# Reading the streamed operand of the weight products from two places in turn, in a two-layer decoder trunk

## The chip, the core and the metric

The kernel runs on one core of a Trainium2 chip. The metric is device time in microseconds (us) of one execution. The engines meant below are PE (TensorE, matrix products), DVE (VectorE), ACT (ScalarE), POOL (GpSimd) and SP, which issues the loads.

## What is computed

Two layers over 272 tokens (16 learned meta tokens ahead of 256 real ones) of width 2048, float32 throughout. Each layer adds a mixer and then a SwiGLU to the residual, each between two RMS norms; the meta tokens are dropped at the end.

```python
for l in range(DEPTH):                       # 2 layers
    hn = rms_norm(h, ln_mix_pre[l])
    mix = mixer_ab(hn, ...) if l % 2 == 0 else mixer_cd(hn, ...)
    h = h + rms_norm(mix, ln_mix_post[l])
    hn = rms_norm(h, ln_ffn_pre[l])
    h = h + rms_norm(swiglu(hn, ffn_w1[l], ffn_w3[l], ffn_w2[l]), ln_ffn_post[l])
return h[:, N_META:]
# swiglu: (silu(h @ w1) * (h @ w3)) @ w2, hidden width 5632
# mixer_ab: h @ w_in (7168 columns) -> gated linear recurrence | short convolution -> @ w_out
# mixer_cd: h @ w_in (4432 columns) -> gated recurrence | sparse attention -> @ w_out
```

## The kernel before

Features lie on the 128 partitions and tokens along the row. The residual is 16 tiles of 128 features by 272 tokens. A product with a weight matrix keeps a 128x128 block of the weight still in the array (the stationary operand) and streams the activations past it: one column of the array's input for each token, 272 of them, or 256 where the meta tokens aren't needed any more. The result goes to a PSUM bank in the order of the tokens.

Each float32 operand x is split into hi, its rounded form in the type fp32r that the array takes in one pass, and lo = x - hi. A product is then three: hi*hi, hi*lo and lo*hi, added up in PSUM. `group` issues them (L189 to L191) for the two 128-feature outputs of a 256-column piece of weight, over all 16 blocks of input features (or fewer for the second SwiGLU matrix). Weights are loaded by SP in pieces of 128x1024 and split by ACT (`whi`, L117) and DVE (`wlo`, L118).

The streamed activations are made in two places. `pre` makes `xh` (ACT) and `xl` (DVE) of the residual, block by block, at the start of each of the four stages (mixer, SwiGLU, mixer, SwiGLU), just ahead of the products that read them; `ahead` and `split_ahead` do the same for eight blocks whose products are issued before the norm is known. `split` makes the two parts of every other operand: gated outputs `og`, convolution outputs `yb`, attention `att`, recurrence `hc` and the SwiGLU's hidden blocks `hid`.

In layer 1 the second SwiGLU matrix is multiplied the other way round (`by_tokens`): the hidden block is the stationary operand, 128 tokens at a time, and the weights are streamed, 512 columns a product (256 for the last two pieces), so that tokens come out on the partitions. `output_part` adds the three partial sums, and `finish` normalizes each block of 128 tokens, adds the residual and stores it.

The order of PE's instructions is the order of the code; a scheduler orders the other engines.

Of the kernel before, what the change touches and what calls it, by code (L numbers as in the profile page):

```python
# [8 lines left out]
F32 = mybir.dt.float32  # L9
# [6 lines left out]
P = 128  # L16
NM = 16
# [24 lines left out]


class Trunk:


# [116 lines left out]
    def group(self, parts, xs, n, pump=0, hooks=None, before=None, between=None, begun=None):  # L163
# [7 lines left out]
        for ci, (k0, kc) in enumerate(self.chunks(parts, nk)):  # L171
# [3 lines left out]
            def products(i, kk):  # L175
# [92 lines left out]
    def spread(self, r, n):  # L268
# [5 lines left out]
        return ps  # L274

    def pre(self, k, lo_t, layer, which, update, xs):

# [57 lines left out]
    def start_stage(self, m, parts1, parts2, lo_t, layer, which, n, factors, update=None, between=None):  # L335
# [8 lines left out]
        def before(k):  # L344
            self.pre(k, lo_t, layer, which, update, xs)
            xg.append(tuple(x[:, nn - n :] for x in xs[k]))

# [24 lines left out]
    def split_ahead(self, m, layer, which, lo_t):  # L372

        nc = self.nc
        for k in range(4):
            g = self.gain(which, layer, k)
            for j, src in (2, self.h[k][:, lo_t:T]), (3, m["m"][k][:, : T - lo_t]):
                xh, xl = self.xhi[j][:, k, lo_t:T], self.xlo[j][:, k, lo_t:T]
                nc.scalar.activation(xh, src, AF.Copy, scale=g)
                nc.vector.scalar_tensor_tensor(xl, src, g, xh.bitcast(F32), op0=ALU.mult, op1=ALU.subtract)  # L380

    def ahead(self, m, parts, n, nn):
# [7 lines left out]
        def products():  # L390
            for accs, j in (near, 2), (far, 3):
                for k in range(kc):
                    xh, xl = self.xhi[j][:, k, T - n : T], self.xlo[j][:, k, T - n : T]
                    for (c, _), a in zip(outs, accs):
                        for i, (w, x) in enumerate(((hi, xh), (hi, xl), (lo, xh))):
                            nc.tensor.matmul(a[:, :n], lhsT=w[:, k, c : c + P], rhs=x, start=k + i == 0,  # L396
                                             stop=accs is far and k == kc - 1 and i == 2)
                            yield
# [359 lines left out]
    def mixer_ab(self, a, fetch, turn, update):  # L758
# [53 lines left out]
        for cp in range(4):  # L812
# [18 lines left out]
            for j in range(2):  # L831
                yb = ys[j]
                V.tensor_tensor(yb, accs[j][:, :T], yb, op=ALU.mult)
                ins[8 + 2 * cp + j] = self.split(yb, T, "yb")
        for hp in range(4):
# [10 lines left out]
            for j in range(2):  # L846
                o = normed[2 * hp + j]
                V.tensor_tensor(o, o, zs[j], op=ALU.mult)
                ins[2 * hp + j] = self.split(o, T, "og")
        order = list(range(8, 16)) + list(range(8))  # L850
        return self.project(a["ab_w_out"][0], [ins[i] for i in order], order, T, 0)

    def project(self, w, ins, order, n, layer):

        xs = [(h[:, :n], l[:, :n]) for h, l in ins]

# [13 lines left out]
    def swiglu(self, a, layer, lo_t, m, out=None):  # L870
# [17 lines left out]
        def hidden(zs, accs, hid):  # L888
# [5 lines left out]
            for y, z in zip(ys, zs):  # L894
                V.tensor_tensor(z, z, y, op=ALU.mult)
                h, l = self.split(z, n, "hid")
                hid.append((h[:, :n], l[:, :n]))

# [121 lines left out]
    def attend(self, h, q, k, vs, bias, out):  # L1020
# [37 lines left out]
        nc.tensor.matmul(last, lhsT=vC[:48, hc], rhs=few[:48].rearrange("p (b c) -> p b c", b=2), start=False, stop=True)  # L1058
        out[h] = self.split(po[:, :NL], NL, "att")
        yield  # L1060

    def mixer_cd(self, a, m):
# [27 lines left out]
        Rr = R[:, NM:T]  # L1090
        xr = [(h[:, NM:T], l[:, NM:T]) for h, l in xs]
        index_queries(accs1 + accs2)
# [79 lines left out]
        for g in range(2):  # L1172
            raw = self.fetch([(0, 0, wuv[:, 512 * g : 512 * (g + 1)].rearrange("(k p) c -> p k c", p=P))], 2, 512)
            hi, lo = self.whole(raw, 2, 512)
            for i, (t0, n) in enumerate(TOK[T]):
                ps = self.pp.tile([P, 512], F32, tag="ps", name="vacc")
                for kk in range(2):
                    ch, cl = cx[kk]
                    nc.tensor.matmul(ps[:n, :], lhsT=ch[:, t0 : t0 + n], rhs=hi[:, kk, :], start=kk == 0, stop=False)
                    nc.tensor.matmul(ps[:n, :], lhsT=ch[:, t0 : t0 + n], rhs=lo[:, kk, :], start=False, stop=False)  # L1180
                    nc.tensor.matmul(ps[:n, :], lhsT=cl[:, t0 : t0 + n], rhs=hi[:, kk, :], start=False, stop=kk == 1)
                c = slice(512 * g, 512 * (g + 1))
                S.copy(vs[i][32:48, c] if i == 2 else vs[i][:, c], ps[:n, :])
                if i == 1:
                    S.copy(vs[2][:NM, c], ps[:NM, :])
                self.pump(1)
# [8 lines left out]
        for g in range(4):  # L1195
# [11 lines left out]
            for c, y, t in both:  # L1207
# [3 lines left out]
                V.scalar_tensor_tensor(y, hs[c][:, NM:T], 0.5, y, op0=ALU.mult, op1=ALU.mult)  # L1211
                ins[c] = self.split(y, NL, "hc")
        self.flush()
# [5 lines left out]

    def by_tokens(self, w, row0, hid, c0, width, rounds, pump=0):  # L1220

        nk, step = len(hid), CH // width
        parts = {}
        for blocks in rounds:
            accs = [self.pp.tile([P, 512], F32, tag="ps", name="acc") for _ in blocks]
            for ci, k0 in enumerate(range(0, nk, step)):
                kc = min(step, nk - k0)
                if ci not in parts:
                    raw = self.fetch(self.cols(w, c0, width, row0)(k0, kc), kc, width)
                    parts[ci] = self.whole(raw, kc, width)  # L1230
                hi, lo = parts[ci]
                for kk in range(kc):
                    k = k0 + kk
                    for b, a in zip(blocks, accs):
                        xh, xl = (x[:, b * P : (b + 1) * P] for x in hid[k])
                        o = a[:, :width]
                        self.nc.tensor.matmul(o, lhsT=xh, rhs=hi[:, kk, :], start=k == 0, stop=False)  # L1237
                        self.nc.tensor.matmul(o, lhsT=xl, rhs=hi[:, kk, :], start=False, stop=False)  # L1238
                        self.nc.tensor.matmul(o, lhsT=xh, rhs=lo[:, kk, :], start=False, stop=k == nk - 1)  # L1239
                self.pump(pump)  # L1240
            yield from zip(blocks, accs)

    def turn(self, tiles, dst):
# [9 lines left out]
        yield  # L1253

    def output_part(self, a, layer, row0, hid, part, pi, out):

# [32 lines left out]
        def take(b, c, src):  # L1289
            t = part[2 * c + b][:, :half]  # L1290
            V.tensor_tensor(t, src, t, op=ALU.add)
            sq = self.slot("sq")
# [20 lines left out]
        for g in range(3):  # L1313
            for b, acc in self.by_tokens(w, row0, hid, 512 * g, 512, ((0, 1),), 1):
                if g + b == 0:
                    load_gain()
                for c in (2 * g, 2 * g + 1):
                    take(b, c, acc[:, half * (c % 2) : half * (c % 2 + 1)])
        self.flush()
# [42 lines left out]
```

## Time and profile before

| | |
|---|---|
| median of 3 runs | 2424.19 us (2424.02 to 2425.62) |
| the profiled execution's own time | 2426.06 us |
| its span, first to last instruction | 2424.3 us |
| PE busy | 2404.4 us (99%), 18563 matmuls |
| DVE, ACT, POOL busy | 61%, 45%, 4% of the span |
[...]

The profiled execution lies 1.87 us above the median; 1.76 us of its time lie outside its span. A matmul's busy time in the profile overlaps with its neighbours' (a 272-column one is shown as 0.29 us long while the next begins 0.125 us later), so the pace of PE is read from the starts of successive matmuls.

### The profile page before, as it was taken

What the parts mean: (1) busy time and instruction counts of PE and PEld (TensorE: products, weight loads), DVE (VectorE), ACT (ScalarE), POOL (GpSimd) and SP (SyncE); (2) the same over time, 40 slices, a digit from 0 to 9 for tenths busy, and PEclk for the clock granted to TensorE, in tenths of its full rate; (3) what the DMA queues carried; (4) which work ended last, traced back from release to release, by engine and by line L of the source; (5) the groups of instructions that cost most, each with busy time, mean ns of one, the idle gap of its engine ahead of it and who ended that gap; (6) DMA issues with size and microseconds to landing.
All of it is one profiled execution on the core that took longest, in us unless ns stands there. A gap on an engine that the chain in (4) does not pass through costs nothing.

```text
span 2424.3 us, 44974 instructions
## 1 busy us (share of the span) xinstructions
PE 2404.4 (99%) x18563; PEld 2331.7 (96%) x18563; DVE 1489.0 (61%) x2441; ACT 1096.4 (45%) x1628; POOL 107.3 (4%) x142
## 2 busy tenths in 40 slices
PE   9999999999999999999999999999999999999998
PEld 8999999999999999999999998999999899989997
DVE  7767566576554455455557788657755455555655
ACT  5333334454443334344355557555444444434443
POOL 1322100000000000000000000100000000000000
PEclk9999999999999999999999999999999999999999
DMA  8444455646555555565554744454666666666663
GB/s 256 144 143 131 146 159 174 183 124 199 174 177 177 177 175 166 174 187 178 166 170 145 210 123 142 146 183 148 210 190 186 190 190 186 189 191 187 187 196 100
DMA packets 402855, 416.97 MB, mean 172 GB/s; under 512 B 15551, under 2 KB 379562, under 8 KB 402650
## 3 DMA queue, kind: packets, MB, share of 16 engines
q1 hardware_dynamic: 402506, 413.95, 56.0%
q8 instruction: 145, 2.38, 0.4%
q14 instruction: 60, 0.49, 0.1%
q10 hardware_dynamic: 144, 0.15, 0.0%
HBM read 411.95 MB, written 2.10 MB: 171 GB/s over the span
## 4 chain that ended last, share of the span: by engine, by line
PE 65%; issue 30%; DVE 3%; DMA 1%; POOL 1%; ACT 1%; SPq 0%; ACTq 0%; DVEq 0%; POOLq 0%
PE acc L189 21%; PE acc L190 20%; PE acc L191 20%; PE lev L682 1%; POOL rms L263 0%; DVE xl L286 0%; DMA raw<-in_ab_w_in_dram 0%; DVE upd L419 0%; DVE wlo L118 0%; DVE h L420 0%; PE idx L992 0%; DVE preacc L314 0%; PE acc L396 0%; DVE wide L1310 0%; PE qk L1028 0%
## 5 line engine op out<-in xcount | busy, mean ns | idle before, releaser
L118 DVE TENSOR_TENSOR wlo<-raw,whi 128x1024 fp32r<-128x1024 f32 (+2 forms) x791 | 953.8, 1208 | 763.6 <-ACT whi L117 759.4
L117 ACT CAST whi<-raw 128x1024 fp32r<-128x1024 f32 (+2 forms) x791 | 817.1, 1035 | 1176.9 <-PE acc L190 862.1
L189 PE MATMUL acc<-xh,whi 128*128 128x272 f32 (+1 forms) x4248 | 1214.8, 286 | 0.5 <-DVE pt L536 0.3
L190 PE MATMUL acc<-xl,whi 128*128 128x272 f32 (+1 forms) x4248 | 1210.3, 285 | 0.6 <-DVE xl L286 0.2
L191 PE MATMUL acc<-xh,wlo 128*128 128x272 f32 (+1 forms) x4248 | 1206.7, 284 | 0.0
L189 PEld LDWEIGHTS acc<-xh,whi 128*128 128x128 f32 x4248 | 799.3, 188 | 5.0 <-ACT xh L285 0.8
L190 PEld LDWEIGHTS acc<-xl,whi 128*128 128x128 f32 x4248 | 797.5, 188 | 2.6 <-DVE xl L286 1.8
L191 PEld LDWEIGHTS acc<-xh,wlo 128*128 128x128 f32 x4248 | 797.6, 188 | 0.0
L189 PE MATMUL acc<-hidh,whi 128*128 128x272 f32 x704 | 202.9, 288 | 0.0
L190 PE MATMUL acc<-hidl,whi 128*128 128x272 f32 x704 | 202.6, 288 | 0.0
L191 PE MATMUL acc<-hidh,wlo 128*128 128x272 f32 x704 | 202.3, 287 | 0.0
L1237 PE MATMUL acc<-whi,hidh 128*128 128x512 f32 (+1 forms) x380 | 144.0, 379 | 0.0
L1239 PE MATMUL acc<-wlo,hidh 128*128 128x512 f32 (+1 forms) x380 | 143.3, 377 | 0.0
L1238 PE MATMUL acc<-whi,hidl 128*128 128x512 f32 (+1 forms) x380 | 143.2, 377 | 0.0
L190 PEld LDWEIGHTS acc<-hidl,whi 128*128 128x128 f32 x704 | 132.6, 188 | 0.0
L191 PEld LDWEIGHTS acc<-hidh,wlo 128*128 128x128 f32 x704 | 132.6, 188 | 0.0
L189 PEld LDWEIGHTS acc<-hidh,whi 128*128 128x128 f32 x704 | 132.5, 188 | 0.0
L1239 PEld LDWEIGHTS acc<-wlo,hidh 128*128 128x128 f32 x380 | 71.5, 188 | 14.3
L1238 PEld LDWEIGHTS acc<-whi,hidl 128*128 128x128 f32 x380 | 71.4, 188 | 13.7
L1237 PEld LDWEIGHTS acc<-whi,hidh 128*128 128x128 f32 x380 | 71.4, 188 | 13.7
L263 POOL TENSOR_TENSOR rms<-ms,minus_half 128x3 f32<-128x3 f32 (+1 forms) x8 | 16.1, 2014 | 1139.6 <-DVE ms L261 999.6
L892 DVE TENSOR_TENSOR y<-acc,scale 128x272 f32<-128x272 f32 (+1 forms) x88 | 35.1, 433 | 12.0 <-PE acc L191 12.0
(363 smaller groups left out, 2105.6 us busy)
## 6 DMA issues: line engine op xcount, KB each, us to landing
raw<-in_ffn_w_dram SPq DMA_DIRECT2D x518, 512.0 KB, 3.6
raw<-in_ab_w_in_dram SPq DMA_DIRECT2D x110, 512.0 KB, 3.6
raw<-in_cd_w_in_dram SPq DMA_DIRECT2D x68, 512.0 KB, 4.1
raw<-in_ab_w_out_dram SPq DMA_DIRECT2D x28, 512.0 KB, 3.6
raw<-in_cd_w_out_dram SPq DMA_DIRECT2D x28, 512.0 KB, 3.4
raw<-in_ffn_w_dram SPq DMA_DIRECT2D x17, 256.0 KB
raw<-in_ab_w_out_dram SPq DMA_DIRECT2D x8, 256.0 KB, 3.0
raw<-in_cd_w_out_dram SPq DMA_DIRECT2D x8, 256.0 KB, 2.8
```

What stands on the lines that cost most here:

```text
L117: nc.scalar.copy(hi[at], raw[at])
L118: nc.vector.tensor_tensor(lo[at], raw[at], hi[at].bitcast(F32), op=ALU.subtract)
L189: nc.tensor.matmul(o, lhsT=hi[:, kk, c : c + m], rhs=xh, start=k == 0, stop=False)
L190: nc.tensor.matmul(o, lhsT=hi[:, kk, c : c + m], rhs=xl, start=False, stop=False)
L191: nc.tensor.matmul(o, lhsT=lo[:, kk, c : c + m], rhs=xh, start=False, stop=k == nk - 1)
L263: i = self.nc.gpsimd.tensor_tensor(r[:, :w], self.ms[:, :w], self.minus_half[:, :w], op=ALU.pow)
L682: nc.tensor.matmul(ps[:M, j * half : (j + 1) * half], lhsT=k[:, j * P : j * P + M], rhs=upper(qh[:, j * P : (j + 1) * P]), start=True, sto ...
L892: V.tensor_tensor(y, accs[j][:, :n], R[:, :n], op=ALU.mult)
L1237: self.nc.tensor.matmul(o, lhsT=xh, rhs=hi[:, kk, :], start=k == 0, stop=False)
L1238: self.nc.tensor.matmul(o, lhsT=xl, rhs=hi[:, kk, :], start=False, stop=False)
L1239: self.nc.tensor.matmul(o, lhsT=xh, rhs=lo[:, kk, :], start=False, stop=k == nk - 1)
```

## The change

Two views are added. `pairs` is a row in its order, seen as pairs of neighbours; `woven` is a row that is seen as two halves, one element from each in turn.

Every streamed activation is now stored woven: tokens 0, 2, 4, ... in the first half of the row, 1, 3, 5, ... in the second. A product reads it through `woven`, so that tokens pass the array in their old order and PSUM is written as before; but each read is 136 elements of 4 bytes away from the one before (128 where the row has 256 tokens). ACT and DVE, which make `xh`, `xl` and the parts of `split`, now read 4-byte elements in order and write them to the two halves in turn; DVE also reads the hi part back from the two halves. Layer 1's hidden blocks, which are stationary there, stay in order; there the streamed weights are read in turn from the two halves of a 512-column piece (256 elements apart), so that the columns come out in another order, which the readers of PSUM undo with a step of two.

At the end of the program, after the last product of the second block of tokens, `forms` adds 50 products whose result nobody reads: five each of ten orders of reading 272, 256 or 512 columns of a weight piece.

```diff
+def pairs(t):
+    return t.rearrange("p (j a) -> p j a", a=2)
+def woven(t):
+    return t.rearrange("p (a j) -> p j a", a=2)
...
-                    o = a[:m, :n]
+                    o = a[:m, :n] if len(xh.shape) == 2 else pairs(a[:m, :n])
                     nc.tensor.matmul(o, lhsT=hi[:, kk, c : c + m], rhs=xh, start=k == 0, stop=False)
...
-    def split(self, src, n, name):
+    def split(self, src, n, name, weave=False):
...
-        self.nc.scalar.copy(hi[:, :n], src)
-        self.nc.vector.tensor_tensor(lo[:, :n], src, hi[:, :n].bitcast(F32), op=ALU.subtract)
+        if weave:
+            hi, lo, src = woven(hi[:, :n]), woven(lo[:, :n]), pairs(src)
+            at = slice(None)
+        else:
+            at = (slice(None), slice(0, n))
+        self.nc.scalar.copy(hi[at], src)
+        self.nc.vector.tensor_tensor(lo[at], src, hi[at].bitcast(F32), op=ALU.subtract)
...
+    def streamed(self, j, k, lo_t):
+        return (woven(x[j][:, k, :])[:, lo_t // 2 :, :] for x in (self.xhi, self.xlo))
...
-        xh, xl = self.xhi[k // 4][:, k % 4, lo_t:T], self.xlo[k // 4][:, k % 4, lo_t:T]
-        a = nc.scalar.activation(xh, h, AF.Copy, scale=g)
-        v = nc.vector.scalar_tensor_tensor(xl, h, g, xh.bitcast(F32), op0=ALU.mult, op1=ALU.subtract)
+        xh, xl = self.streamed(k // 4, k % 4, lo_t)
+        a = nc.scalar.activation(xh, pairs(h), AF.Copy, scale=g)
+        v = nc.vector.scalar_tensor_tensor(xl, pairs(h), g, xh.bitcast(F32), op0=ALU.mult, op1=ALU.subtract)
...
-                        o = a[:, :width]
-                        self.nc.tensor.matmul(o, lhsT=xh, rhs=hi[:, kk, :], start=k == 0, stop=False)
+                        o, wh, wl = pairs(a[:, :width]), woven(hi[:, kk, :]), woven(lo[:, kk, :])
+                        self.nc.tensor.matmul(o, lhsT=xh, rhs=wh, start=k == 0, stop=False)
...
+    def forms(self, hid):
...
+        far = lambda d, n: f[:, : 2 * d].rearrange("p (a j) -> p j a", a=2)[:, : n // 2, :]
+        for rhs, n in (
+            (f[:, 0:272], 272),
+            (far(128, 256), 256),
+            (far(136, 272), 272),
+            (far(256, 512), 512),
+            (far(240, 272), 272),
+            (far(160, 256), 256),
+            (far(130, 256), 256),
+            (f[:, 0:256].rearrange("p (a j) -> p j a", a=4), 256),
+            (f[:, 0:256].rearrange("p (a j c) -> p j a c", a=2, c=2), 256),
+            (f[:, 0:256].rearrange("p (a j c) -> p j a c", a=2, c=8), 256),
+        ):
...
+            for _ in range(5):
+                self.nc.tensor.matmul(o, lhsT=x, rhs=rhs, start=True, stop=True)
...
-                        src = acc[:, half * (c % 2) : half * (c % 2 + 1)]
+                        src = acc[:, c % 2 : 512 : 2]
...
         for b, acc in self.by_tokens(w, row0, hid, 7 * half, half, ((0,), (1,))):
             take(b, 7, acc[:, :half])
+            if b:
+                self.forms(hid)
             finish(b)
```

No instruction changes its place on any engine, apart from the 50 that are added. On DVE, at the start of layer 0's SwiGLU stage, the program before reads as follows; `upd` and `h` are the update of a residual block, `xl` its lo part.

```order
L419 TENSOR_TENSOR upd<-m,spread 128x272
L420 TENSOR_TENSOR h_121<-h_121,upd 128x272
L419 TENSOR_TENSOR upd<-m,bc 128x272 x2
L286 SCALAR_TENSOR_TENSOR xl<-h_121,pt_107,xh 128x272
L420 TENSOR_TENSOR h_122<-h_122,upd 128x272
```

The same place after the change:

```order
L439 TENSOR_TENSOR upd<-m,spread 128x272
L440 TENSOR_TENSOR h_121<-h_121,upd 128x272
L439 TENSOR_TENSOR upd<-m,bc 128x272 x2
L306 SCALAR_TENSOR_TENSOR xl<-h_121,pt_107,xh 128x136x2
L440 TENSOR_TENSOR h_122<-h_122,upd 128x272
```

Only the shape of `xl` differs: 136 pairs, one element of each in either half. On PE, the end of the program before is this (`acc` is the sum of the last 128x256 piece of the output):

```order
L1238 MATMUL acc<-whi,hidl 128x256
L1239 MATMUL acc<-wlo,hidh 128x256
L1237 MATMUL acc<-whi,hidh 128x256
L1238 MATMUL acc<-whi,hidl 128x256
L1239 MATMUL acc<-wlo,hidh 128x256
L1358 UNCONDITIONAL_BRANCH
```

After the change the same products are followed by the added ones:

```order
L1260 MATMUL acc<-whi,hidl 128x256
L1261 MATMUL acc<-wlo,hidh 128x256
L1301 MATMUL forms<-whi,hidh 128x272 x5
L1301 MATMUL forms<-whi,hidh 128x256 x5
L1301 MATMUL forms<-whi,hidh 128x272 x5
L1301 MATMUL forms<-whi,hidh 128x512 x5
L1301 MATMUL forms<-whi,hidh 128x272 x5
L1301 MATMUL forms<-whi,hidh 128x256 x25
L1411 UNCONDITIONAL_BRANCH
```

Nothing is queued behind them on PE.

## Rows read from the trace of the kernel before

**Rows 1.** The page: span and busy engines (us, share, instructions).
```profile
span 2424.3 us, 44974 instructions
PE 2404.4 (99%) x18563; PEld 2331.7 (96%) x18563; DVE 1489.0 (61%) x2441; ACT 1096.4 (45%) x1628; POOL 107.3 (4%) x142
```

**Rows 2.** Waits of PE: line, whom for, us in total, times, longest.
```profile
PE rgr L952 <- issue: 4.9, 1, 4.9
PE spread L272 <- POOL rms L263: 3.0, 3, 1.9
```

**Rows 3.** Timeline, 272-column products: start us, us, instruction.
```profile
999.72 0.29 PE L191 MATMUL acc<-hidh,wlo 128*128 128x272 f32 x1
...
1003.98 0.29 PE L189 MATMUL acc<-hidh,whi 128*128 128x272 f32 x1
```

**Rows 4.** Timeline, 512-column products followed by 256-column ones.
```profile
2384.79 0.39 PE L1237 MATMUL acc<-whi,hidh 128*128 128x512 f32 x1
...
2395.23 0.28 PE L1237 MATMUL acc<-whi,hidh 128*128 128x256 f32 x1
...
2400.03 0.28 PE L1239 MATMUL acc<-wlo,hidh 128*128 128x256 f32 x1
```

**Rows 5.** Timeline, a plain float32 product of 272 columns, in two passes.
```profile
156.94 0.62 PE L721 MATMUL o<-A,vt 128*128 128x272 f32 x2
157.40 0.41 PE L722 MATMUL o<-A,vt 128*128 128x144 f32 x2
```

**Rows 6.** Stretches of 100 us: engines' busy us (instructions), PE clock, DMA share, GB/s.
```profile
600.00:700.00 100.00, 100.00 (x802) 100.00 (x802) 55.20 (x74) 40.56 (x50) 0.00 (x0) 1.00 0.58 175
700.00:800.00 100.00, 100.00 (x802) 100.00 (x802) 43.38 (x40) 39.49 (x50) 0.00 (x0) 1.00 0.59 178
```

**Rows 7.** Groups of PE's matmuls by shape: count | busy us, mean ns.
```profile
L190 PE MATMUL acc<-xl,whi 128*128 128x272 f32 x2456 | 710.2, 289 | 0.2
...
L190 PE MATMUL acc<-xl,whi 128*128 128x256 f32 x1776 | 495.7, 279 | 0.3 <-DVE xl L286 0.2
...
L189 PE MATMUL acc<-hidh,whi 128*128 128x272 f32 x704 | 202.9, 288 | 0.0
...
L1237 PE MATMUL acc<-whi,hidh 128*128 128x512 f32 x324 | 128.3, 396 | 0.0
...
L189 PE MATMUL acc<-ogh,whi 128*128 128x272 f32 x128 | 37.1, 290 | 0.0
...
L1237 PE MATMUL acc<-whi,hidh 128*128 128x256 f32 x56 | 15.7, 281 | 0.0
```

**Rows 8.** Groups of DVE's instructions by shape, some with stepped operands.
```profile
L705 DVE TENSOR_TENSOR qh<-qh,F 128x136 f32<-128x136 f32 x24 | 9.5, 396 | 0.0
...
L687 DVE COPY_PREDICATED A<-lev,lev 126x128 f32<-126x128 uint8 x8 | 3.6, 452 | 6.6 <-PE lev L685 6.4
L671 DVE COPY_PREDICATED A<-lev,diag 128x128 f32<-128x128 uint8 x8 | 3.6, 446 | 0.0
...
L705 DVE TENSOR_TENSOR qh<-qh,f 128x136 f32<-128x136 f32 x8 | 2.6, 322 | 1.1 <-POOL A L646 1.1
...
L687 DVE COPY_PREDICATED A<-lev,lev 124x128 f32<-124x128 uint8 x8 | 2.4, 297 | 7.1 <-PE lev L685 6.9
```

**Rows 9.** One of six stretches of 25 us, and the sum over all six.
```profile
1675.00:1700.00 25.00, 24.86 (x209) 24.40 (x208) 25.00 (x60) 18.19 (x38) 0.00 (x0) 1.00 0.34 106
sum 150.00, PE 144.08 PEld 139.69 DVE 144.71 ACT 93.21 POOL 25.60; mean PE 24.01 PEld 23.28 DVE 24.12 ACT 15.53 POOL 4.27
```

**Rows 10.** Timeline: the last `xl` of a stage, and the products that first read it.
```profile
531.85 0.51 DVE L286 SCALAR_TENSOR_TENSOR xl<-h,pt,xh 128x272 fp32r<-128x272 f32 x1
...
536.74 0.29 PE L190 MATMUL acc<-xl,whi 128*128 128x272 f32 x1
```

**Rows 11.** Timeline: PE's last matmul, and the last instruction on DVE.
```profile
2414.96 0.28 PE L1239 MATMUL acc<-wlo,hidh 128*128 128x256 f32 x1
...
2419.70 0.74 DVE L1310 SCALAR_TENSOR_TENSOR wide<-m,rms,wide 128x512 f32<-128x512 f32 x1
```

More of the change, by code (lines that the diff above doesn't have):

```diff
@@ L345, in before @@
             self.pre(k, lo_t, layer, which, update, xs)
-            xg.append(tuple(x[:, nn - n :] for x in xs[k]))
+            xg.append(tuple(x[:, (nn - n) // 2 :, :] for x in xs[k]))
         accs1 = self.group(parts1, xg, n, before=before, between=between, begun=begun)
@@ L392, in products @@
                 for k in range(kc):
-                    xh, xl = self.xhi[j][:, k, T - n : T], self.xlo[j][:, k, T - n : T]
+                    xh, xl = self.streamed(j, k, T - n)
                     for (c, _), a in zip(outs, accs):
                         for i, (w, x) in enumerate(((hi, xh), (hi, xl), (lo, xh))):
-                            nc.tensor.matmul(a[:, :n], lhsT=w[:, k, c : c + P], rhs=x, start=k + i == 0,
+                            nc.tensor.matmul(pairs(a[:, :n]), lhsT=w[:, k, c : c + P], rhs=x, start=k + i == 0,
                                              stop=accs is far and k == kc - 1 and i == 2)
@@ L853, in project @@
     def project(self, w, ins, order, n, layer):
-        xs = [(h[:, :n], l[:, :n]) for h, l in ins]
+        xs = ins
         def cols(c0, width):
@@ L895, in hidden @@
                 V.tensor_tensor(z, z, y, op=ALU.mult)
-                h, l = self.split(z, n, "hid")
-                hid.append((h[:, :n], l[:, :n]))
+                hid.append(tuple(x[:, :n] for x in self.split(z, n, "hid")) if out is not None else self.split(z, n, "hid", True))
         for pi, (f0, f1) in enumerate(FPARTS):
@@ L1058, in attend @@
         nc.tensor.matmul(last, lhsT=vC[:48, hc], rhs=few[:48].rearrange("p (b c) -> p b c", b=2), start=False, stop=True)
-        out[h] = self.split(po[:, :NL], NL, "att")
+        out[h] = self.split(po[:, :NL], NL, "att", True)
         yield
@@ L1090, in mixer_cd @@
         Rr = R[:, NM:T]
-        xr = [(h[:, NM:T], l[:, NM:T]) for h, l in xs]
+        xr = [tuple(x[:, NM // 2 :, :] for x in both) for both in xs]
         index_queries(accs1 + accs2)
@@ L1178, in mixer_cd @@
                     ch, cl = cx[kk]
-                    nc.tensor.matmul(ps[:n, :], lhsT=ch[:, t0 : t0 + n], rhs=hi[:, kk, :], start=kk == 0, stop=False)
-                    nc.tensor.matmul(ps[:n, :], lhsT=ch[:, t0 : t0 + n], rhs=lo[:, kk, :], start=False, stop=False)
-                    nc.tensor.matmul(ps[:n, :], lhsT=cl[:, t0 : t0 + n], rhs=hi[:, kk, :], start=False, stop=kk == 1)
+                    o, wh, wl = pairs(ps[:n, :]), woven(hi[:, kk, :]), woven(lo[:, kk, :])
+                    nc.tensor.matmul(o, lhsT=ch[:, t0 : t0 + n], rhs=wh, start=kk == 0, stop=False)
+                    nc.tensor.matmul(o, lhsT=ch[:, t0 : t0 + n], rhs=wl, start=False, stop=False)
+                    nc.tensor.matmul(o, lhsT=cl[:, t0 : t0 + n], rhs=wh, start=False, stop=kk == 1)
                 c = slice(512 * g, 512 * (g + 1))
-                S.copy(vs[i][32:48, c] if i == 2 else vs[i][:, c], ps[:n, :])
+                S.copy(woven(vs[i][32:48, c] if i == 2 else vs[i][:, c]), pairs(ps[:n, :]))
                 if i == 1:
-                    S.copy(vs[2][:NM, c], ps[:NM, :])
+                    S.copy(woven(vs[2][:NM, c]), pairs(ps[:NM, :]))
                 self.pump(1)
@@ L1231, in by_tokens @@
                 hi, lo = parts[ci]
+                self.flat = hi.rearrange("p k c -> p (k c)")
                 for kk in range(kc):
@@ L1253, in turn @@
         yield
+    def forms(self, hid):
+        f = self.flat
+        x = hid[0][0][:, :P]
+        ps = self.misc("forms")
+        far = lambda d, n: f[:, : 2 * d].rearrange("p (a j) -> p j a", a=2)[:, : n // 2, :]
[11 more added lines that the diff above has]
+        ):
+            o = ps[:, :n]
+            if len(rhs.shape) == 3:
+                o = o.rearrange("p (j a) -> p j a", a=rhs.shape[2])
+            elif len(rhs.shape) == 4:
+                o = o.rearrange("p (j a c) -> p j a c", a=2, c=rhs.shape[3])
+            for _ in range(5):
+                self.nc.tensor.matmul(o, lhsT=x, rhs=rhs, start=True, stop=True)
     def output_part(self, a, layer, row0, hid, part, pi, out):
@@ L1290, in take @@
             t = part[2 * c + b][:, :half]
-            V.tensor_tensor(t, src, t, op=ALU.add)
+            if c < 6:
+                V.tensor_tensor(t, src, t, op=ALU.add)
+            else:
+                V.tensor_tensor(woven(t), pairs(src), woven(t), op=ALU.add)
             sq = self.slot("sq")
@@ L1317, in output_part @@
                 for c in (2 * g, 2 * g + 1):
-                    take(b, c, acc[:, half * (c % 2) : half * (c % 2 + 1)])
+                    take(b, c, acc[:, c % 2 : 512 : 2])
         self.flush()
```

16 lines of the change are left out of this document (8 added, 8 removed).

## The prediction, as it was put on record

> **What bounds the kernel.** I read the page first: PE is busy for 2404.4 of 2424.3 us [rows 1]. Then its waits: the longest is 4.9 us and the next sums to 3.0 [rows 2]. So the time is the number of matmuls times the pace at which PE starts them, and only that pace can move it by much. A matmul's shown duration overlaps with the next one, so the pace is read from starts. For 272 columns, 34 intervals lie between 999.72 and 1003.98: 125.3 ns each [rows 3]. For 512 columns there are 45 intervals from 2384.79 to 2395.23, 232.0 ns each, and for 256 columns 41 from there to 2400.03, 117.1 ns each [rows 4]. From 256 to 512 a column costs (232.0 - 117.1) / 256 = 0.449 ns, and 117.1 - 256 x 0.449 = 2.2 ns are fixed. [...]
>
> Is that another engine in the way? In the stretch 600 to 700 DVE is busy for 55.2 us and in 700 to 800 for 43.4, and both show the same 802 matmuls [rows 6]. So it isn't DVE; the two stretches move data alike, 175 and 178 GB/s. [...]
>
> **The change, part by part.**
>
> *The order of reading.* This is the term that decides. Counts: at 272 columns three groups of 2456 with `xh` and `xl`, three of 704 with `hid`, six of 128 (`og`, `yb`), together 10248; at 256 columns three of 1776, six of 128 (`att`, `hc`), three of 56, together 6264; at 512 columns three of 324, 972 [rows 7]. A rest of some 280 products is left out. At today's pace they take 10248 x 125.3 + 6264 x 117.1 + 972 x 232.0 ns = 1284.1 + 733.5 + 225.5 = 2243 us. No row shows PE reading single elements from two places in turn, so the price is bounded from both sides.
>
> [...] If the two are fetched independently, a column costs 0.417 ns and the fixed 2.2 stay: 115.5, 108.9 and 215.5 ns. The saving is 10248 x 9.8 + 6264 x 8.2 + 972 x 16.5 ns = 100.4 + 51.4 + 16.0 = 168 us.
>
> Upper end: if what is fetched for one place is lost at the switch to the other, each column pays for a fetch. The nearest rows with broken runs are DVE's: a predicated copy of 128 elements takes 297 ns with runs of four, but 452 with runs of two and 446 with single ones (L687, L671), 1.2 ns more an element [rows 8]. On PE that would be 0.449 + 1.2 = 1.65 ns a column, or 1.2 x (10248 x 272 + 6264 x 256 + 972 x 512) ns = 5870 us more.
>
> [...]
>
> I take the lower end. [...] But I hold this with little more than even odds.
>
> *Where DVE can't follow.* In six stretches of 25 us DVE is busy for 144.71 of 150 us [rows 9]: there it paces the kernel, or nearly, and a faster PE would wait. PE's 144 us in them don't shrink by 168 / 2243 = 7.5%: 10.8 us of the saving are not had.
>
> *Making the woven operands.* Some 160 instructions on DVE and as many on ACT now write in turn to two places. A DVE row with every second element in and out takes 322 ns for 136 elements, less than the 396 of the same line's forms with longer runs (L705), so the cost may be nothing; by the predicated copies it is 1.2 x 272 = 0.33 us an instruction at most [rows 8]. Where DVE is 61% busy or less this is hidden behind PE's products. In the four passes of `pre` it isn't wholly: 16 `xl` each, one for each block of features. The last `xl` of such a pass ends at 532.36 and is first read at 536.74, 4.4 us later [rows 10]. A faster PE eats 16 blocks x 12 products x 9.8 ns = 1.9 us of it, and 16 x 0.33 = 5.3 us at the most go to DVE: 0 to 2.8 us a pass in three passes, and 0 to 5.3 in the first, which has no such slack. Together 0 to 14 us; I take 5. If that cover were gone altogether, 4 x 5.3 = 21 us.
>
> *The 50 unused products.* They are 15 of 272, 30 of 256 and 5 of 512 columns: at today's pace 1.9 + 3.5 + 1.2 = 6.6 us. PE's last product starts at 2414.96, and DVE, ACT, POOL and the stores then work until 2424.3 [rows 1, 11]. PE would be done near 2421.7, hidden behind that tail, with 2.6 us to spare. At 1.65 ns a column the 45 that aren't in order take some 20 us, and they would end the kernel.
>
> *The tail.* The last addition from PSUM is woven too, 0 to 0.3 us on the path: 0.2. The reads of PSUM with a step of two (28 adds and 16 copies) come while PE goes on with the next piece; they are hidden.
>
> Sum against the profiled execution's span: 2424.3 - 168 + 10.8 + 5 + 0.2 = 2272.3 us. With the 1.76 us outside the span that is 2274.1, and the median lies 1.87 lower than that execution: **2272 us**.
>
> **The rivals.**
>
> [...]
>
> [...]
>
> *Each switch costs a fetch* (slower). It happens at the streamed operand of each product, and it decides as soon as a column costs over 0.449 ns. For it: DVE's broken runs [rows 8]. Against it: DVE's row L705 with steps of two shows no such price. By the upper end: 2424 + 5870 + some 13 for the unused products at the end = 8310 us; with only one column in two delayed, 5370 us.
>
> **Chances.** The whole saving 0.50, half of it 0.13, no change in pace 0.17, a fetch at each switch 0.20. In the third, 0.10 falls within 0.2% (4.8 us, about what a measurement of this kernel can tell from no change) and 0.07 above it. So faster 0.63, same 0.10, slower 0.27. The range for 8 in 10 covers the first three: from 2255, where nothing of the saving is given back, to 2436. Of the likeliest alone it is 2255 to 2300.
>
> **What the profile after would show.** Right: starts of 272-column products 115 to 116 ns apart, some 865 instead of 802 in a stretch of 100 us; DVE waits where there were none and PE waits for `xl` or `wlo` of some us at the stage starts. [...] What would make me wrong above all is that the delivery is bound by each fetch and not by the stream; next, that DVE, with more work and less time, becomes the bound in more than these six stretches.

## The result, and the profile after

| | before | after |
|---|---|---|
| median | 2424.38 us (4 runs, 2424.02 to 2425.62) | 2306.46 us (4 runs, 2306.19 to 2310.25) |
| span of the profiled execution | 2424.3 us | 2308.5 us |
| ratio | 1 | 0.9516 (0.9500 to 0.9533) |

The change makes the kernel 4.8% faster. The forecast was 2272 us; the result lies 34 us above it and outside the range of the likeliest case alone (2255 to 2300), but inside the whole range. The profiled execution is the slowest of the four, some 4 us above the others.

The page of the changed kernel (as rows 1): PE has 50 products more and is busy for 127 us less, DVE and ACT are busy for 22 and 31 us more.

```profile
span 2308.5 us, 45101 instructions
PE 2277.6 (99%) x18613; PEld 2217.1 (96%) x18613; DVE 1511.5 (65%) x2441; ACT 1127.6 (49%) x1628; POOL 109.7 (5%) x142
```

The timeline of the changed kernel, PE: 272-column products, answering to rows 3. Between these two starts lie 45 intervals, 115.8 ns each instead of 125.3.

```profile
939.74 0.28 PE L202 MATMUL acc<-hidh,wlo 128*128 128x272 f32 x1
...
944.95 0.28 PE L202 MATMUL acc<-hidh,wlo 128*128 128x272 f32 x1
```

The same view of 512 and 256 columns, answering to rows 4. There are 30 intervals between the first two rows, 215.7 ns each (232.0 before), and 49 between the last two, 111.6 ns each (117.1 before).

```profile
2259.52 0.38 PE L1261 MATMUL acc<-wlo,hidh 128*128 128x512 f32 x1
...
2265.99 0.38 PE L1261 MATMUL acc<-wlo,hidh 128*128 128x512 f32 x1
...
2282.71 0.28 PE L1261 MATMUL acc<-wlo,hidh 128*128 128x256 f32 x1
...
2288.18 0.28 PE L1259 MATMUL acc<-whi,hidh 128*128 128x256 f32 x1
```

The two stretches of rows 6 after the change: 866 products instead of 802 in 100 us.

```profile
600.00:700.00 100.00, 100.00 (x866) 100.00 (x865) 58.38 (x72) 45.08 (x54) 0.00 (x0) 1.00 0.62 190
700.00:800.00 100.00, 100.00 (x866) 100.00 (x865) 49.56 (x50) 43.46 (x54) 0.00 (x0) 1.00 0.63 190
```

With the counts of rows 7 the pace alone is worth 10248 x 9.5 + 6264 x 5.5 + 972 x 16.3 ns = 97.4 + 34.5 + 15.8 = 147.7 us. The medians differ by 117.9. So 29.8 us of it were given back (16.0 were forecast). The waits of PE after the change (line, whom for, us in total, times, longest), answering to rows 2, say where to look:

```profile
PE spread L288 <- POOL rms L279: 9.5, 3, 3.6
PE acc L201 <- DVE xl L306: 7.1, 20, 0.9
PE rgr L971 <- issue: 6.0, 1, 6.0
...
PE acc L200 <- ACT xh L305: 1.5, 6, 0.4
```

Both grown waits, for `rms` and for `xl` and `xh`, belong to the starts of the stages, where the residual and its split are made just ahead of the products. The stage start of layer 0's SwiGLU lies between 475 and 550 us in both kernels. The table of stretches there (PE, PEld, DVE, ACT, POOL busy us, clock, DMA share, GB/s), first the kernel before, then the changed one:

```profile
475.00:550.00 75.00, 74.47 (x591) 73.53 (x590) 54.50 (x102) 41.13 (x70) 4.66 (x3) 1.00 0.49 152
```

```profile
475.00:550.00 75.00, 69.18 (x547) 66.34 (x547) 60.17 (x115) 42.08 (x67) 5.80 (x3) 0.95 0.46 141
```

At 866 products in 100 us there would be 649 in these 75 us; 547 were made. 102 are missing, 11.8 us. (Before, 591 of 601, 1.2 us.) Of the 11.8, 3.6 are the wait for `rms`, and 2.9 are a lower clock behind it, shown below. The rest, some 5 us, lies where products wait for `xl` and `xh`: the starts there are 4.9 us further apart in all than usual. (The list of waits has less for them, since it counts only the time in which PE is shown idle.) Adding up for the whole trace what each interval between the starts of two products exceeds the usual one of its shape, I find two further places like it: 1225 to 1300 (some 12 us) and 1575 to 1650 (some 11 us). The three together lost some 34 us, and some 6 before.

Here is the wait in the timeline of the changed kernel (start us, us, engine, line, operation; in brackets the idle time before it and who ended it):

```profile
514.36 0.63 PE L262 MATMUL stat<-ones,preacc 128*128 128x1 f32 x6
517.20 0.20 DVE L275 TENSOR_SCALAR ms<-stat 128x2 f32<-128x2 f32 x2
517.33 3.47 DVE L129 TENSOR_TENSOR wlo<-raw,whi 128x1024 fp32r<-128x1024 f32 x3
517.48 4.04 POOL L279 TENSOR_TENSOR rms<-ms,minus_half 128x3 f32<-128x3 f32 x1 [40.02 <-DVE ms L275]
517.69 0.28 PE L202 MATMUL acc<-xh,wlo 128*128 128x272 f32 x1
521.57 0.90 PE L288 MATMUL spread<-ident,rms 128*128 128x128 f32 x3 [3.61 <-POOL rms L279]
...
522.79 0.43 PE L201 MATMUL acc<-xl,whi 128*128 128x272 f32 x1
...
525.97 0.43 PE L200 MATMUL acc<-xh,whi 128*128 128x272 f32 x1
```

Four steps in a row: PE's sums `stat` are there at 515.0; DVE gets to `ms` at 517.20, behind three `wlo`; POOL needs 4.04 us for `rms`; PE starts the last of its products at 517.69 and then idles for 3.61 us. Behind the wait there are 14 intervals between the last two rows, 227 ns each: there the granted clock is 0.50, as the stretches below show.

The same place in the kernel before, where PE waited for 0.48 us:

```profile
544.11 0.63 PE L246 MATMUL stat<-ones,preacc 128*128 128x1 f32 x6
545.17 0.21 DVE L259 TENSOR_SCALAR ms<-stat 128x2 f32<-128x2 f32 x2
545.31 2.34 DVE L118 TENSOR_TENSOR wlo<-raw,whi 128x1024 fp32r<-128x1024 f32 x2
545.46 2.90 POOL L263 TENSOR_TENSOR rms<-ms,minus_half 128x3 f32<-128x3 f32 x1 [36.27 <-DVE ms L259]
548.42 0.59 PE L272 MATMUL spread<-ident,rms 128*128 128x128 f32 x3 [0.48 <-POOL rms L263]
```

So the wait grew by 3.1 us, and only 0.2 of it is PE passing the 24 products between `stat` and the spread faster (2.86 instead of 3.08 us from start to start). `ms` comes 2.2 instead of 0.4 us after `stat` (1.8 us), and `rms` takes 4.04 instead of 2.90 us (1.1 us), with a third `wlo` directly behind the second. At the third place `rms` goes from 1.65 to 5.01 us, and PE, which didn't wait there before, waits for 3.24:

```profile
1703.52 1.65 POOL L263 TENSOR_TENSOR rms<-ms,minus_half 128x2 f32<-128x2 f32 x1 [33.87 <-DVE ms L259]
```

```profile
1620.02 5.01 POOL L279 TENSOR_TENSOR rms<-ms,minus_half 128x2 f32<-128x2 f32 x1 [37.28 <-DVE ms L275]
```

The clock, in the view of stretches for PE alone (busy us and products, clock, DMA share, GB/s): 0.50 is already granted in the last microsecond of the wait, and holds for 5.83 us behind it, which at 227 instead of 115.8 ns a product costs half of them, 2.9 us.

```profile
520.60:521.57 0.97, 0.00 (x0) 0.50 1.03 362
521.57:527.40 5.83, 5.83 (x25) 0.50 0.90 292
```

How long the woven operands take to make, in the groups by shape: the kernel before (us in total, mean ns, idle before),

```profile
L285 ACT ACTIVATE xh<-h,pt 128x272 fp32r<-128x272 f32 x32 | 15.6, 518 | 12.2 <-DVE h L420 12.0
L286 DVE SCALAR_TENSOR_TENSOR xl<-h,pt,xh 128x272 fp32r<-128x272 f32 x32 | 15.0, 495 | 0.0
L220 ACT CAST hidh<-z 128x272 fp32r<-128x272 f32 x44 | 16.3, 415 | 0.0
```

and after:

```profile
L305 ACT ACTIVATE xh<-h,pt 128x272 fp32r<-128x272 f32 x32 | 22.6, 770 | 15.3 <-DVE h L440 15.1
L306 DVE SCALAR_TENSOR_TENSOR xl<-h,pt,xh 128x272 fp32r<-128x272 f32 x32 | 21.0, 707 | 2.5 <-ACT xh L305 1.4
L236 ACT CAST hidh<-z 128x272 fp32r<-128x272 f32 x44 | 26.1, 692 | 0.3 <-DVE z L915 0.3
L237 DVE TENSOR_TENSOR hidl<-z,hidh 128x272 fp32r<-128x272 f32 x44 | 25.0, 647 | 0.0
```

DVE pays 0.21 us an instruction, ACT 0.25 to 0.28.

The 50 unused products stand beside the tail, answering to rows 11: the first starts at 2298.57, the last at 2305.16, while DVE's last instruction begins at 2303.85 and the kernel ends at 2308.5.

```profile
L1301 PE MATMUL forms<-whi,hidh x50: 273/284/380, 2298.6 to 2305.2; 128*128 128x256 f32 x30, 128*128 128x272 f32 x15, 128*128 128x512 f32 x5
2303.85 0.74 DVE L1361 SCALAR_TENSOR_TENSOR wide<-m,rms,wide 128x512 f32<-128x512 f32 x1
```

Their starts in the trace, five of each order, mean ns from one to the next:

| order | columns | ns |
|---|---|---|
| in order | 272 | 126 |
| two places 128, 130 or 160 apart | 256 | 111 to 112 |
| two places 136 or 240 apart | 272 | 116 |
| two places 256 apart | 512 | 216 |
| four places 64 apart | 256 | 143 |
| two places 128 apart, runs of two | 256 | 168 |
| two places 128 apart, runs of eight | 256 | 124 |

### The profile page after: what moved, and what is told of

It is laid out like the page before. It is cut to its first block, busy times and chain, and to the rows that moved or that the text cites. A ratio compares the mean times of both kernels' runs of the same rounds, so it can differ in the third digit from the quotient of the medians.

```text
span 2308.5 us, 45101 instructions
## 1 busy us (share of the span) xinstructions
PE 2277.6 (99%) x18613; PEld 2217.1 (96%) x18613; DVE 1511.5 (65%) x2441; ACT 1127.6 (49%) x1628; POOL 109.7 (5%) x142
## 4 chain that ended last, share of the span: by engine, by line
PE 94%; DVE 3%; ACT 1%; POOL 1%; issue 1%; DMA 0%; SPq 0%; DVEq 0%
PE acc L200 27%; PE acc L201 26%; PE acc L202 26%; PE acc L1261 3%; PE acc L1260 3%; PE acc L1259 3%; DVE xl L306 1%; ACT xh L305 1%; PE lev L702 1%; POOL rms L279 1%; DVE h L440 0%; DVE wlo L129 0%; PE idx L1011 0%; PE forms L1301 0%; PE acc L416 0%
## 5 line engine op out<-in xcount | busy, mean ns | idle before, releaser
L200 PE MATMUL acc<-xh,whi 128*128 128x272 f32 (+1 forms) x4248 | 1193.5, 281 | 3.7 <-DVE pt L556 1.8
L201 PE MATMUL acc<-xl,whi 128*128 128x272 f32 (+1 forms) x4248 | 1184.6, 279 | 7.2 <-DVE xl L306 7.1
L202 PE MATMUL acc<-xh,wlo 128*128 128x272 f32 (+1 forms) x4248 | 1182.2, 278 | 0.0
L201 PEld LDWEIGHTS acc<-xl,whi 128*128 128x128 f32 x4248 | 811.2, 191 | 11.9 <-DVE xl L306 11.3
L200 PEld LDWEIGHTS acc<-xh,whi 128*128 128x128 f32 x4248 | 811.2, 191 | 9.5 <-ACT xh L305 3.9
L202 PEld LDWEIGHTS acc<-xh,wlo 128*128 128x128 f32 x4248 | 811.3, 191 | 0.0
L200 PE MATMUL acc<-hidh,whi 128*128 128x272 f32 x704 | 196.7, 279 | 0.0
L201 PE MATMUL acc<-hidl,whi 128*128 128x272 f32 x704 | 196.6, 279 | 0.0
L202 PE MATMUL acc<-hidh,wlo 128*128 128x272 f32 x704 | 196.6, 279 | 0.0
L305 ACT ACTIVATE xh<-h,pt 128x272 fp32r<-128x272 f32 (+1 forms) x48 | 33.5, 760 | 22.2 <-DVE h L440 21.7
```

The source lines that it names most:

```text
L305: a = nc.scalar.activation(xh, pairs(h), AF.Copy, scale=g)
```

## The experiments

My theory after this: the pace is won by reading alternately, and what was given back at the stage starts comes from the dearer making of the woven operands. Rivals: the cost lies in something else that the faster PE runs into, or the pace isn't everywhere what the last 50 products show.

### Parts of the change alone

**e3_split_only** stores and reads `xh` and `xl` in order; all else stays as in the change.

```diff
-        return (woven(x[j][:, k, :])[:, lo_t // 2 :, :] for x in (self.xhi, self.xlo))
+        return (x[j][:, k, lo_t:T] for x in (self.xhi, self.xlo))
...
-        a = nc.scalar.activation(xh, pairs(h), AF.Copy, scale=g)
+        a = nc.scalar.activation(xh, h, AF.Copy, scale=g)
...
```

> xh and xl are stored and read in order again; all other streamed operands stay woven. If the order of reading sets the pace and the parts add up, the 7368 products of 272 and 5328 of 256 columns with xh and xl go back to 125.3 and 117.1 ns, which gives back 7368 x 9.5 + 5328 x 5.4 ns = 99 of the 147 us that the pace saved, and PE's waits at the stage starts go with the making of xh and xl; so 2424.4 - 48 = 2376, 2372 to 2381 us. Rival: the woven storage of hid, og, yb, att and hc costs DVE and ACT so much that it eats its own saving: 2395 or more.

Measured: 2378.25 us (2376.69 to 2378.97), ratio 0.9802 (0.9788 to 0.9817) to the kernel before, 2425.79 us in these runs. The pace sum without `xh` and `xl` (3 x 2456 products of 272 columns, 3 x 1776 of 256) is 147.7 - 70.0 - 29.3 = 48.4 us, which gives 2377.4: only 0.9 us was given back, and the time lies in the expected range. So the 29.8 us hang on `xh` and `xl`, their making or their pace; weaving the other operands costs nothing that can be seen, though `hidh` and `hidl` take half as long again and more (716 for 415 ns, 664 for 434).

**e4_weights_only** is the kernel before, where only `by_tokens` reads its weights from two places. Nothing is stored differently; the columns come out in another order, and the readers of PSUM undo that with a step of two, as in the change (that part of the edit isn't shown).

```diff
-                        o = a[:, :width]
-                        self.nc.tensor.matmul(o, lhsT=xh, rhs=hi[:, kk, :], start=k == 0, stop=False)
+                        o, wh, wl = pairs(a[:, :width]), woven(hi[:, kk, :]), woven(lo[:, kk, :])
+                        self.nc.tensor.matmul(o, lhsT=xh, rhs=wh, start=k == 0, stop=False)
...
```

> Only the streamed weights of layer 1's second SwiGLU matrix are read from two places; they are stored in order, as before, and nothing is made differently. If the order of reading alone sets the pace, the 972 products of 512 columns begin every 215.8 ns instead of 232 and the 168 of 256 columns every 111.7 instead of 117.1: 16.6 us less, 2406 to 2409 us. Rival: it is the woven storage and not the order of reading that helps; then 232 ns stay and the time is 2424 to 2426.

Measured: 2409.99 us (2408.39 to 2410.91), ratio 0.9933 (0.9918 to 0.9948), 15.8 us less than before. The sum of its 972 and 168 products is 15.8 + 0.9 = 16.7 us. That is what the order of reading gives, with the step of two in PSUM's readers as the only other edit. The time lies 1 us above the expected range, which was worked out from 2424.4 us for the kernel before; here that kernel took 2425.79.

### Cheaper making: right in kind, and only a third of it

**e1_halves** lets ACT and DVE write each woven row half after half in order, and read the source with a step of two instead. The operands and the products are those of the change.

```diff
+def halves(t):
+    return t.rearrange("p j a -> p a j")
...
-        a = nc.scalar.activation(xh, pairs(h), AF.Copy, scale=g)
-        v = nc.vector.scalar_tensor_tensor(xl, pairs(h), g, xh.bitcast(F32), op0=ALU.mult, op1=ALU.subtract)
+        hp = halves(pairs(h))
+        a = nc.scalar.activation(halves(xh), hp, AF.Copy, scale=g)
+        v = nc.vector.scalar_tensor_tensor(halves(xl), hp, g, halves(xh).bitcast(F32), op0=ALU.mult, op1=ALU.subtract)
```

> ACT and DVE write each woven row half by half, in order, and read their source with a step of two; the products are those of the changed kernel. If the waits of PE at the three stage starts (34 us over the usual pace in the changed kernel, 6 in the one before) come from the dearer making of xh and xl (ACT 518 to 770 ns, DVE 495 to 707), both fall back under 560 ns, the half-clock stretches after these waits go, and the median comes to 2283 to 2293 us. Rival: the waits come from PE's faster pace against a DVE that was full already; then the median stays within 2303 to 2308, whatever the making costs. Second rival: reading with a step of two costs as much as writing to two places; then ACT and DVE stay above 650 ns and the median at 2306.

Measured: 2297.47 us (2294.93 to 2302.70), ratio 0.9472 (0.9457 to 0.9488). This is 9 us below the change (10.4 us, if each is set against the kernel before in its own runs), and above the 2283 to 2293 us of the theory. Its groups by shape show that the price of making is gone: `xl` 500 ns, `xh` 551.

```profile
L313 ACT ACTIVATE xh<-h,pt 128x272 fp32r<-128x272 f32 x32 | 16.6, 551 | 12.6 <-DVE h L449 12.4
L314 DVE SCALAR_TENSOR_TENSOR xl<-h,pt,xh 128x272 fp32r<-128x272 f32 x32 | 15.3, 500 | 0.0
```

So dear making was one part of the cause, and 2297.47 - (2425.79 - 147.7) leaves 19.4 us of give-back. Its waits of PE show the other part: those for `xl` fell from 7.1 to 1.6 us, and the one for `rms` stayed.

```profile
PE spread L295 <- POOL rms L286: 10.1, 4, 3.7
...
PE acc L206 <- DVE xl L314: 1.6, 4, 0.7
```

In its timeline the stage start reads as in the change, some 4 us earlier: `ms` comes late, behind three `wlo`, and is followed by three more, `rms` takes 4.04 us beside them, and the spread waits. Cheaper making doesn't shorten this.

```profile
513.40 0.20 DVE L282 TENSOR_SCALAR ms<-stat 128x2 f32<-128x2 f32 x2
513.54 3.47 DVE L134 TENSOR_TENSOR wlo<-raw,whi 128x1024 fp32r<-128x1024 f32 x3
513.69 4.04 POOL L286 TENSOR_TENSOR rms<-ms,minus_half 128x3 f32<-128x3 f32 x1 [36.23 <-DVE ms L282]
517.78 0.59 PE L295 MATMUL spread<-ident,rms 128*128 128x128 f32 x3 [3.69 <-POOL rms L286]
```

I then formed the theory that PE, being faster, runs through the products between `stat` and the spread before `rms` is there, and loses clock after the wait. (By the rows above most of it is the other side: `ms` and `rms` come later.)

### Giving PE work until rms is there

**e5_later_spread** is e1_halves without the unused products, and takes the next group of products, which the code issued right after the stage start anyway, ahead of the spread. (The text below says five stage starts; the edit reaches the three that follow a residual update, which are the three places above.)

```diff
-        accs2 = self.group(parts2, xg, n, hooks=dict(enumerate(steps)))
-        return xs, got, accs1, accs2
+        accs2 = self.group(parts2, xg, n, hooks=dict(enumerate(steps[:3] if m else steps)))
+        if not m:
+            return xs, got, accs1, accs2
+        accs3 = self.group(parts3, xg, n, hooks={1: steps[3]})
+        return xs, got, accs1, accs2, accs3
...
-                hidden(zs, self.group([self.pair(w3, 2 * P)], xs, n), hid)
+                hidden(zs, accs3, hid)
```

> The kernel of e1_halves without the fifty unused products, and at each of the five stage starts one more group of products is issued ahead of the spread of the rms row, which the products had to wait for: some 5.6 us of products more stand between the last row's squares and the spread. Theory (what e1_halves did not win back is PE waiting for POOL's row rms at the stage starts, 4 waits of 10.1 us in all, and the clock of one half behind them): these waits fall to 0 to 1 us in all, and the time to 2283 to 2288 us. Rival (VectorE has no time to spare there, so that the wait only moves to the row xl or to the groups behind): the spread's waits go, others of the same size take their place, and the time stays at 2294 to 2298 us. Without the unused products alone, nothing changes, since they ran behind the last group's tail.

Measured: 2283.10 us (2282.39 to 2284.59), ratio 0.9413 (0.9401 to 0.9426), the fastest version. The wait for `rms` is gone. Apart from `rgr`, which has 4.9 us in the kernel before and 6.0 in the change, no wait sums to more than 1.9 us:

```profile
PE rgr L983 <- issue: 6.0, 1, 6.0
PE acc L206 <- DVE xl L314: 1.9, 6, 0.7
PE acc L205 <- ACT xh L313: 1.6, 2, 1.1
```

The instructions ahead of the spread haven't become faster. `rms` still takes 4.04 us beside `wlo`, but ends at 518.54, and the spread comes at 520.29 without idle time:

```profile
514.50 4.04 POOL L286 TENSOR_TENSOR rms<-ms,minus_half 128x3 f32<-128x3 f32 x1 [36.23 <-DVE ms L282]
520.29 0.54 PE L295 MATMUL spread<-ident,rms 128*128 128x128 f32 x3
```

The stretch 475 to 550, first of e1_halves, then of e5_later_spread: 589 and 637 products, and with the wait gone the clock is 1.00 instead of 0.98.

```profile
475.00:550.00 75.00, 71.06 (x589) 69.86 (x589) 59.47 (x117) 40.80 (x69) 5.80 (x3) 0.98 0.49 152
```

```profile
475.00:550.00 75.00, 74.76 (x637) 73.75 (x637) 62.30 (x123) 42.98 (x72) 5.80 (x3) 1.00 0.53 164
```

Of the pace's 147.7 us this version gives back 2283.1 - (2425.38 - 147.7) = 5.4.

**e7_before_later_spread** makes the same edit in the kernel before, with all operands in order, to see whether it is worth as much at the old pace.

> The kernel before, all operands in order, with only the later spread of e5_later_spread at the three stage starts that have a group to put ahead of it. Theory (the wait for POOL's rms is what the faster PE ran into, and is worth in the kernel before only the 3.0 us that it waited there): 2421 to 2424 us. Rival (the later spread is worth its 14 us whatever the pace, so that e5_later_spread says nothing of the change): 2411 us.

Measured: 2423.22 us (2422.42 to 2424.65), ratio 0.9992 (0.9982 to 1.0001), 2.5 us less than before, by the interval 4.4 at most, and as forecast. The three waits of 3.0 us [rows 2] have 2.4 us at the places that the edit reaches; at the new pace the same edit is worth 14 us, with the clock that it saves. So most of this wait came with the change.

**e6_no_forms** is the change without `forms` and its call.

> The changed kernel without its fifty unused products, nothing else changed. Theory (they ran while the other engines worked on the last block's tail): the time stays that of the changed kernel, 2306 to 2310 us. Rival (their 6.6 us lay on the path): 2300 us.

Measured: 2308.28 us (2305.93 to 2310.51), ratio 0.9521 (0.9505 to 0.9537), the time of the change. The 50 products are hidden behind the tail, as forecast. The profiled execution took 2305.93 us, and in it the three places lose some 31 us; so some 3 of the 34 us above belong to the slower execution that was profiled there.

### The orders of reading by themselves

**p1_orders** and **p2_more_orders** are the changed kernel with other unused products at the end, 24 of each order, and were executed once each; only the starts of these products count here, not the time of the whole.

```diff
+        two = lambda d, n: f[:, :n].rearrange("p (b a j) -> p b j a", a=2, j=d) if n > 2 * d else woven(f[:, :n])
+        way = lambda n, **k: f[:, :n].rearrange("p (a j c) -> p j a c", **k)
...
+            (two(4, 512), 512, P, None),
...
+            (way(512, a=2, c=4), 512, P, None),
```

> The changed kernel, with 24 unused products for each of 13 orders at its end in place of the 50; its time says nothing, the starts of these products do. In order, 512 columns: 232 ns. From two places 256 apart: 215.8. In order with a stationary operand of 32 columns instead of 128: 232 if the stream's own delivery is late; 216 if its reads collide with those of the weight load. Two places 256, 64, 8, 4 and 2 elements apart: if two fetches under way at once are what helps, 216 for those that lie in different 16-byte pieces (4 and up) and 232 or more for 2; rival: only far places help, and 4 and 8 are over 232. Every second element of 1024: twice the bytes, so 2 x 0.449 x 512 + 2 = 460 ns if delivery is by 16-byte pieces, 232 if by elements. One element repeated: 216. 256 columns, 128-column stationary: 117 in order and 112 from two places; with 96 stationary columns 117 and, if the 112 is the weight load's own time, 109; rival: 112 again, if it is the read's.

> Six groups of 24 unused products of 512 columns at the kernel's end, each in another order of reading: from two places 256 elements apart in runs of 2, 4 and 8 elements, from 4 places and from 8 places in turn, and in order. Theory A (a product gains only where two successive elements lie in different pieces of 16 bytes, whatever the number of places): runs of 2, 4 and 8 lie between 216 and 233 ns, 4 and 8 places at 216 ns. Theory B (each further step of the reading order costs something by itself, as the fifty products of the changed kernel showed: runs of 2 took 168 ns and four places 143 ns at 256 columns): runs of 2 take some 330 ns, 4 places some 280 ns, 8 places as much or more; runs of 8 near 240 ns.

Start to start, the mean of 23 intervals, a weight of 128 columns unless said otherwise:

| order | columns | ns |
|---|---|---|
| in order (p1, p2) | 512 | 232.6, 234.5 |
| in order, weight of 32 columns | 512 | 230.7 |
| two places 256, 64, 8 or 4 elements apart | 512 | 215.8, 215.9, 215.8, 215.7 |
| two places 2 apart | 512 | 234.1 |
| one element again and again | 512 | 218.6 |
| every second of 1024 elements, in order | 512 | 452.2 |
| four places; eight places | 512 | 273.3; 488.6 |
| two places, runs of 2, 4, 8 | 512 | 328.9, 249.5, 243.4 |
| in order | 256 | 118.8 |
| in order, weight of 96 columns | 256 | 120.0 |
| two places | 256 | 111.5 |
| two places, weight of 96 columns | 256 | 109.2 |

A stretch of p1_orders shows it by count (PE busy us and products, clock, DMA share, GB/s): 71 products in 15 us for the three groups with two places 4, 8 and 64 apart.

```profile
2328.00:2343.00 15.00, 15.00 (x71) 1.00 0.01 1
```

What follows: a weight of 32 columns instead of 128 changes little in order (230.7 for 232.6 ns), so a collision with its loading isn't shown, nor one with DMA (two places 2 apart are as slow, 234.1 ns, and the DMA share beside them is 0.00). Two places 4 elements (16 bytes) apart, read in turn, are enough for the whole gain; 2 elements apart there is none. p1_orders came out as expected but for small misses: one element again and again takes 218.6 and not 216 ns, and 256 columns in order take 118.8 and 120.0 and not 117. Theory B of p2_more_orders holds in its numbers, though eight places are far dearer than the 280 ns that it gave as their least: runs, and more than two places, are slower than reading in order. Theory A is out. And at 256 columns from two places the product falls with a weight of 96 columns, which also leaves 96 rows of output, from 111.5 to 109.2 ns, against the forecast 108.9; I read this as another limit there.

## Why the prediction was right, and where its sizes were off

**The bound and the direction: right.** PE's pace was the bound, it went with the columns, and reading from two places in turn brings it down: 115.8 for the forecast 115.5 ns at 272 columns, 215.7 for 215.5 at 512, from 125.3 and 232.0 in order [rows 3, 4]. e4_weights_only shows it with nothing else changed but the readers of PSUM. The first unused products, in order, stood 126 ns apart, those behind them, from two places, 111 to 112 at 256 columns, 116 at 272 and 216 at 512. No run shows where the sum's 0.417 ns a column comes from; what the runs showed in its place, with two places, is (115.8 - 2.2) / 272 = 0.418 and (215.7 - 2.2) / 512 = 0.417 ns, but (111.6 - 2.2) / 256 = 0.427. That two places are fetched independently, as the lower end supposes, isn't borne out as a reason: by it any two places should have done well, and four too, but two places 2 elements apart take 234.1 ns and four places 273.3. That the change used two places, and not near ones, was luck as far as that reason goes.

**The term "saving, 168 us" was mis-sized at 256 columns.** I let the fixed part and 0.417 ns a column set the pace of every shape. At 256 columns it was 111.6 instead of 108.9 ns: 6264 x 2.7 ns = 17 us; 272 columns missed by 0.3 ns, 3 us. p1_orders shows that the same product comes to 109.2 ns with a weight of 96 columns, which leaves 96 rows of output as well. That the weight load is the floor, there and in the kernel (111.5 and 111.6 ns), is my inference; it wasn't tried by itself. These 20 us and the next term's 14 make up the 34 us between forecast and result.

**The terms "DVE-full stretches, 10.8" and "making, 5" were mis-sized together: 16.0 forecast, 29.8 measured.** That DVE would hold up the faster PE at the stage starts, and with waits for `xl`, was right. That a full DVE holds PE up wherever it is full was not. Of the six stretches of rows 9, three (525 to 550, 1325 to 1350 and 1675 to 1700) lie at the three places, and the one from 1450 to 1475 lost some 3 us more than before. But in the two from 25 to 75 the program lost only 0.6 us more, where the term had 3.6: PE starts 407 products instead of 382, beside a DVE that is busy for 49.78 of 50 us. The table of stretches, before and after:

```profile
25.00:75.00 50.00, 49.10 (x382) 47.46 (x381) 47.97 (x133) 28.10 (x51) 16.94 (x18) 1.00 0.73 229
```

```profile
25.00:75.00 50.00, 48.23 (x407) 46.96 (x406) 49.78 (x134) 28.43 (x49) 15.72 (x19) 1.00 0.71 226
```

Three things were left out. The making of `xh` by ACT has a price as well (0.25 us), and DVE's `xl` waits for it; DVE's price of 0.21 us lay in my bounds, but row L705, by which I leaned to nothing [rows 8], was a bad guide: e1_halves shows that reading with a step is nearly free (`xl` 500 ns for 495) and that the price comes with going to two places in turn (707). For ACT, which only writes so, that is the writing (`xh` 770 ns, 551 in e1_halves); DVE also reads the hi part back so, and which of the two it pays for wasn't separated. Second, I priced the slack of `xl` [rows 10] and not that of `rms`, although the wait for it was the second line of rows 2: DVE reaches `ms` later after `stat`, and `rms` itself takes longer beside a longer run of `wlo`; that the products between pass faster is the least of it, 0.2 us of 3.1 at the place shown. Third, the granted clock of 0.50 that came with the wait: 2.9 us behind it at that place. e1_halves won back 10 of the 29.8 us and e5_later_spread 14 more; 5.4 are left.

**The rival "each switch costs a fetch"** stayed on DVE's rows and didn't come to PE with two places, 215.7 ns for 512 columns against 232.6 in order. Other orders are dearer than in order: four places take 273.3 ns, eight 488.6, runs of two 328.9; what they pay for, no run shows. The rivals "half of it" and "no change in pace" are excluded by rows of every shape; the least of the saving, 5.5 of 8.2 ns, is that at 256 columns.

**The unused products:** hidden, as forecast (e6_no_forms).

**Open.** Why `rms` takes 4.04 us here and 0.86 at 476.59, in the same kernel and on the same 128x3 elements, wasn't tried by itself. The traces show a pattern: at 476.59 no `wlo` runs beside it, and where one does, at the stage starts behind a residual update, `rms` ends 0.56 to 0.71 us after the end of one of them, in every kept trace: of the first (it then takes 1.65 or 1.78 us), the second (2.90), the third (3.97, 4.04) or the fourth (4.37 to 5.02). No run here shows the cause. Nor was it tried why DVE has more `wlo` to do at once at these starts when PE is faster. Open, too, is why two places in turn are read faster than in order and four slower (215.7, 232.6 and 273.3 ns for 512 columns). Reading in turn from operands stored in order, with PSUM written in two halves, wasn't tried.

## What to carry to other kernels

Before pricing a change of pace, work out each shape's pace against every limit it may meet, the next one included: here one product shape got two thirds of the gain (5.5 of 8.2 ns), and in p1_orders a narrower weight took it from 111.5 to 109.2 ns. When the bound engine gets faster, go through its short waits in the trace before, and ask for each how many products stand between the cause and the wait, and what else will queue up on the engines that answer. Two of the three new stalls had been waits of 0.5 and 1.9 us; the third had been none, with 0.7 us to spare. Moving work that was ready ahead of them was worth 14 us here. When a layout must change, let the writer go through memory in order and the reader step: here that took `xl` from 707 to 500 ns and `xh` from 770 to 551.

## What the runs showed that I hadn't expected

- PE streams fp32r faster from two places in turn, 4 elements (16 bytes) or more apart (215.7 ns for 512 columns), than in order (232.6) or from a single element (218.6).
- Runs make it worse: two places in runs of two, four and eight elements take 328.9, 249.5 and 243.4 ns, all slower than in order.
- Writing 4-byte elements to two places in turn costs ACT 0.25 to 0.28 us on 272 elements, and DVE, which also reads one operand from two places in turn, 0.21 us; reading with a step of two costs 5 ns on DVE and 33 on ACT (`xl` 500 for 495, `xh` 551 for 518).
- POOL's power of 128x3 elements took 0.86 us and 4.04 us in one kernel; the longer ones end 0.6 to 0.7 us after one of DVE's back-to-back `wlo`.
